# A decoder layer's SwiGLU halves: the down products of the four plain tiles moved directly behind them, in four parts instead of three

## The chip, the cores and the metric

The program runs on one core of one Trainium2 chip. The metric is the device time of one execution in microseconds (us). TensorE is PE in the profile (its weight loads PEld), VectorE is DVE, ScalarE is ACT, GpSimd is POOL, and SyncE is SP, which issues most of the loads.

## The reference

One layer over 512 tokens of width 1024, all in float32. The change lies in the two SwiGLU halves, one at each end of the layer; between them are the HGRN2 and convolution groups and the cross-attention.

```python
def swiglu(h, w_gate, w_up, w_down):
    return (jax.nn.silu(h @ w_gate) * (h @ w_up)) @ w_down

x = x + 0.5 * swiglu(rms_norm(x, ffn1_norm[l]), ffn1_gate[l], ffn1_up[l], ffn1_down[l])
...
x = x + 0.5 * swiglu(rms_norm(x, ffn2_norm[l]), ffn2_gate[l], ffn2_up[l], ffn2_down[l])
return rms_norm(x, final_norm)
```

The hidden width is 2816, which is 22 tiles of 128.

## The kernel before, in words

Every float32 operand is split in two parts that add up to it: a high part made by ACT (`whi`, `ah`, `a11h`, ...) and a low part made by DVE as the difference (`wlo`, `al`, `a11l`, ...). A product takes three matmuls: high by high, high by low, low by high (`mm3`, lines 119 to 121; line 339 for the block products). So each weight costs a load by DMA into a `raw` tile, a conversion by ACT and a subtraction by DVE. `wpool` has three buffers each of `raw`, `whi` and `wlo`; a `whi` buffer is written again once PE has done with it.

A half (`class Half`) makes its 22 hidden tiles in two ways. Tiles 0 to 3 are plain (`CLASSIC = 4`): `product(m, j)` multiplies the normed input by the gate weights (j = 0) or the up weights (j = 1), 24 matmuls of 512 columns, and `finish(m, ps)` scales by the row norm `bc`, applies silu, multiplies, and splits the result into the hidden tile (`ah`, `al`). Tiles 4 to 21 come in pairs from seven 2x2 block products (`seven(m)`: p1, p5, r6, p2, r7, p4, p3, each 24 matmuls of 256 columns). Their moving operands are combinations of the scaled input, made once per half by `inputs_steps()`: `xa` (line 253), `tx`, the differences q1 and n2, the combinations `tc`, and from these seven pairs of split inputs (`quad`, lines 242 and 243: a11, q1, n2, a12, d3, a22, q4). Their weights are five tiles per pair of hidden tiles, loaded by `load(m)` into six buffers with the tag `raw` in the pool `hp`: b11, t1 (loaded, then a second block added to it by a POOL DMA), b22, b21, t3 (a POOL load and a POOL add).

The down projection runs in parts of the hidden tiles (`PARTS`): `down_tile` loads the weights of one of the eight output tiles for one part, multiplies into a PSUM bank `psd`, and `residual` (line 192) adds the bank to `x` on DVE. [...] Before, the first part is hidden tiles 0 to 7, in the pair m = 8.

The order on each engine is set by the scheduler from the order of the code and its own estimates: an instruction may be put ahead of another, and from then on each engine works through its list strictly in order. In `run`, the plain tiles come first, the input steps stand among them, and the last input steps (`later`) stand among the first pair's seven products. In the first half a special `first_tile` makes three products at once while x arrives; the sum of squares of x (`Norm.add`) and two small mask loads (`mskf`, converted by DVE) stand behind it.

Of the kernel before, what the change touches and what calls it, by code (L numbers as in the profile page):

```python
# [8 lines left out]
F32 = mybir.dt.float32  # L9
# [29 lines left out]
def decoder_layer(ctx: ExitStack, tc: tile.TileContext, xT, memT, vecs, masks, ident_d,  # L39
                  w1, w1d, w_in, w_i, w_out, w_q, w_k, w_v, w_o, w2, w2d, gfin, out):  # L40
    nc = tc.nc
# [3 lines left out]
    tmp = ctx.enter_context(tc.tile_pool(name="tmp", bufs=2))  # L45
# [3 lines left out]
    def bank(name):  # L49
        return psp.tile([P, 512], F32, tag="ps", name=name)  # L50
# [65 lines left out]
    def mm3(out, wh, wl, xh, xl, first, last):  # L116


        nc.tensor.matmul(out, lhsT=wh, rhs=xh, start=first, stop=False)  # L119
        nc.tensor.matmul(out, lhsT=wh, rhs=xl, start=False, stop=False)  # L120
        nc.tensor.matmul(out, lhsT=wl, rhs=xh, start=False, stop=last)  # L121
# [69 lines left out]
    def residual(ps, k, scale):  # L191
        nc.vector.scalar_tensor_tensor(x[k], ps, scale, x[k], op0=ALU.mult, op1=ALU.add)  # L192


    CLASSIC = 4
    PARTS = ((0, 8), (8, 16), (16, FT))

    class Half:

# [46 lines left out]
        def inputs_steps(self):  # L246

            name, hp = self.name, self.hp
            self.q, later = {}, []
            sub = lambda o, a, b: nc.vector.tensor_tensor(o, a, b, ALU.subtract)  # L250

            def scaled(t, k):
                nc.vector.scalar_tensor_tensor(t, x[k], vec[:, self.gcol + k:self.gcol + k + 1], self.bc,
                                               op0=ALU.mult, op1=ALU.mult)

            self.tx = [hp.tile([P, 2, S], F32, tag=t, name=f"x{t}_{name}", bufs=4) for t in ("ah", "al")]
            self.tc = [hp.tile([P, 2, S], F32, tag=t, name=f"c{t}_{name}", bufs=4) for t in ("ah", "al")]
            steps = []
            for n in range(2):
                xb, comb = self.tx[n], self.tc[n]  # L260
                xa = []

                def one(n=n, xb=xb, xa=xa):
                    xa.append(hp.tile([P, 2, S], F32, tag="g", name=f"xa_{name}{n}", bufs=1))
                    for i in range(2):
                        scaled(xa[0][:, i], 2 * n + i)
                    self.quad("a11", n, xa[0][:, :, :256])

                def two(n=n, xb=xb, xa=xa):
                    for i in range(2):  # L270
                        scaled(xb[:, i], 4 + 2 * n + i)
                    q1 = tmp.tile([P, 2, 256], F32, tag="sq", name=f"q1_{name}{n}")
                    sub(q1, xa[0][:, :, 256:], xb[:, :, 256:])
                    self.quad("q1", n, q1)
                    n2 = tmp.tile([P, 2, 256], F32, tag="t2", name=f"n2_{name}{n}")
                    sub(n2, q1, xa[0][:, :, :256])
                    self.quad("n2", n, n2)
                    self.n2 = n2

                def three(n=n, xb=xb, comb=comb, xa=xa):  # L280
                    d3, q4 = comb[:, :, :256], comb[:, :, 256:]
                    sub(d3, xa[0][:, :, :256], xa[0][:, :, 256:])
                    nc.vector.tensor_tensor(q4, xb[:, :, :256], self.n2, ALU.add)
# [109 lines left out]
            return p1, p5, r6, p2, r7, p4, p3  # L393


        def run(self, first, down, fill, last):
# [12 lines left out]
            self.finish(2, p2)  # L409
            p3 = []  # L410
            for j in range(2):
                steps.pop(0)()
                steps.pop(0)()
                p3.append(self.product(3, j))
            self.finish(3, p3)
            for s in steps:
                s()
            before = None
            for m in range(CLASSIC, FT, 2):
                p1, p5, r6, p2, r7, p4, p3 = self.seven(m)  # L420
# [5 lines left out]
                for s in later[:2]:  # L426
                    s()
                r6()
                for s in later[2:4]:
                    s()  # L430
                part = [q for q, (a, b) in enumerate(PARTS) if b == m]
                if part:
                    down(part[0])
                p2()
                for s in later[4:6]:
                    s()
                r7()
                for s in later[6:]:
                    s()
                later = []  # L440
# [6 lines left out]
    def down_tile(half, name, d, part, src, n0=0, n1=None, p=None):  # L447
# [52 lines left out]
    with tc.tile_pool(name="hid1", bufs=1, reuse_waits="tile") as hp:  # L500
        half = Half("f1", hp, xs, norm, w1, V_FFN1)

        def src1(d, k0, k1):
            return w1d[d, :, k0 * P:k1 * P]

        def down1(part):
            for d in range(KT):
                down_tile(half, "f1", d, part, src1)

        L0, L1 = PARTS[-1]  # L510
        LATE = FT - 2
        psl = {}

        def early1(d):


            w = (LATE - L0) * P
            wh, wl = weights(w1d[d:d + 2, :, L0 * P:LATE * P].rearrange("d p c -> p d c"), (2, w))
            for i in range(2):
                p = psl[d + i] = bank(f"psd_f1l{d + i}")  # L520
                for k in range(L0, LATE):
                    hi, lo = half.hidden(k)
                    c = slice((k - L0) * P, (k - L0 + 1) * P)
                    mm3(p, wh[:, i, c], wl[:, i, c], hi, lo, k == L0, False)

        def fill1():
            early1(0)

        def last1():
            early1(2)  # L530
            wh, wl = weights(w1d[:4, :, LATE * P:].rearrange("d p c -> p d c"), (4, 2 * P))
            for d in range(4):
                for k in range(LATE, FT):
                    hi, lo = half.hidden(k)
                    c = slice((k - LATE) * P, (k - LATE + 1) * P)
                    mm3(psl[d], wh[:, d, c], wl[:, d, c], hi, lo, False, k == FT - 1)
                residual(psl[d], d, 0.5)
                done_m(d)
            for d in range(4, KT):
                down_tile(half, "f1", d, 2, src1)  # L540
                done_m(d)

        half.run(first_tile, down1, fill1, last1)


    norm_a, xs_a, done_a = prepare(V_XATT, "xa")
    with tc.tile_pool(name="mix", bufs=8, reuse_waits="tile") as mp:
# [26 lines left out]
        f = big("f")  # L574
# [92 lines left out]
        fill = []  # L667
# [297 lines left out]
    with tc.tile_pool(name="hid2", bufs=1, reuse_waits="tile") as hp:  # L965
# [3 lines left out]
        def src2(d, k0, k1):  # L969
            return w2d[k0:k1, :, d * P:(d + 1) * P].rearrange("k p c -> p k c")  # L970

        def down2(part):
            for d in range(KT):
                down_tile(half, "f2", d, part, src2)
# [9 lines left out]
        half.run(None, down2, fill2, lambda: None)  # L984
# [131 lines left out]
```

## Time and profile before

| what | value |
| --- | --- |
| runs shown | 1128.27 us median of 3 (1126.99 to 1129.56) |
| profiled execution, its own time | 1127.54 us |
| span of the profile, first to last instruction | 1125.8 us |
| mean granted TensorE clock | 0.990 |
| PE / DVE / ACT / POOL busy | 98% / 64% / 43% / 7% |
| DMA | 140.53 MB, mean 125 GB/s |

The time of the profiled execution is 1.7 us more than its span, and 0.7 us below the median of the runs. Times of rows are us from the span's start. A timeline row gives start, duration, engine, line, operation, output<-inputs, shapes and, in brackets, the idle time of the engine before it with what ended it. The matmul rows overlap, since matmuls are pipelined: what one costs in a stream is the distance from one start to the next.

### The profile page before, as it was taken

What the parts mean: (1) busy time and instruction counts of PE and PEld (TensorE: products, weight loads), DVE (VectorE), ACT (ScalarE), POOL (GpSimd) and SP (SyncE); (2) the same over time, 40 slices, a digit from 0 to 9 for tenths busy, and PEclk for the clock granted to TensorE, in tenths of its full rate; (3) what the DMA queues carried; (4) which work ended last, traced back from release to release, by engine and by line L of the source; (5) the groups of instructions that cost most, each with busy time, mean ns of one, the idle gap of its engine ahead of it and who ended that gap; (6) DMA issues with size and microseconds to landing.
All of it is one profiled execution on the core that took longest, in us unless ns stands there. A gap on an engine that the chain in (4) does not pass through costs nothing. (4 is left out here: it accounts for less than half of the span.)

```text
span 1125.8 us, 15892 instructions
## 1 busy us (share of the span) xinstructions
PE 1101.7 (98%) x6528; PEld 983.2 (87%) x6528; DVE 719.7 (64%) x956; ACT 486.1 (43%) x659; POOL 75.7 (7%) x75
## 2 busy tenths in 40 slices
PE   8979999999999999999999999999799999999997
PEld 6879889998998888888889888888699899988995
DVE  5797447754667575885776456553986366734744
ACT  6355325542445343323464345342654145523553
POOL 1001001100100000000100000000011011100102
PEclk9989999999999999999999999999999999999999
DMA  9428537773523322322234424732257357653521
GB/s 325 144 57 203 134 97 183 170 187 93 141 63 101 110 94 75 95 75 84 66 113 132 131 75 150 205 94 83 68 132 193 90 140 200 164 145 105 126 75 75
DMA packets 69641, 140.53 MB, mean 125 GB/s; under 512 B 4816, under 2 KB 22480, under 8 KB 69568
## 3 DMA queue, kind: packets, MB, share of 16 engines
q1 hardware_dynamic: 55008, 108.02, 31.1%
q0 software_dynamic: 12544, 28.84, 13.0%
q10 hardware_dynamic: 2016, 2.66, 0.7%
q8 instruction: 51, 0.84, 0.3%
q14 instruction: 22, 0.18, 0.0%
HBM read 137.40 MB, written 2.10 MB: 124 GB/s over the span
## 5 line engine op out<-in xcount | busy, mean ns | idle before, releaser
L110 ACT ACTIVATE whi<-raw 128x1024 fp32r<-128x1024 f32 (+4 forms) x135 | 136.5, 1016 | 337.4 <-PE psd_f L120 90.7
L111 DVE TENSOR_TENSOR wlo<-raw,whi 128x1024 fp32r<-128x1024 f32 (+4 forms) x135 | 157.2, 1168 | 87.8 <-ACT whi L110 87.4
L317 ACT ACTIVATE whi<-b_f 128x1024 fp32r<-128x1024 f32 x72 | 76.4, 1061 | 113.2 <-PE psd_f L120 35.0
L318 DVE TENSOR_TENSOR wlo<-b_f,whi 128x1024 fp32r<-128x1024 f32 x72 | 88.1, 1224 | 36.2 <-ACT whi L317 35.1
L119 PE MATMUL psd_f<-ah_f,whi 128*128 128x512 f32 x280 | 109.0, 389 | 0.0
L120 PE MATMUL psd_f<-al_f,whi 128*128 128x512 f32 x280 | 109.0, 389 | 0.0
L121 PE MATMUL psd_f<-ah_f,wlo 128*128 128x512 f32 x280 | 108.9, 389 | 0.0
L192 DVE SCALAR_TENSOR_TENSOR xall<-psd_f,xall 128x512 f32<-128x512 f32 x36 | 24.9, 692 | 103.6 <-PE psd_f L121 103.6
L318 DVE TENSOR_TENSOR wlo<-t_f,whi 128x1024 fp32r<-128x1024 f32 x54 | 66.1, 1224 | 36.7 <-ACT whi L317 36.7
L317 ACT ACTIVATE whi<-t_f 128x1024 fp32r<-128x1024 f32 x54 | 57.1, 1058 | 49.6 <-issue 20.8
L121 PEld LDWEIGHTS psd_f<-ah_f,wlo 128*128 128x128 f32 x280 | 52.6, 188 | 11.0
L119 PEld LDWEIGHTS psd_f<-ah_f,whi 128*128 128x128 f32 x280 | 52.6, 188 | 10.8
L120 PEld LDWEIGHTS psd_f<-al_f,whi 128*128 128x128 f32 x280 | 52.6, 188 | 10.7
L339 PE MATMUL psD_f<-q1h_f,wlo 128*128 128x256 f32 x144 | 42.8, 297 | 4.9 <-DVE wlo L318 4.9
L339 PE MATMUL psA_f<-a11h_f,whi 128*128 128x256 f32 x144 | 41.9, 291 | 5.6 <-ACT a11h_f L242 5.6
L339 PE MATMUL psA_f<-a11l_f,whi 128*128 128x256 f32 x144 | 42.2, 293 | 1.6 <-DVE a11l_f L243 1.6
L339 PE MATMUL psD_f<-q1l_f,whi 128*128 128x256 f32 x144 | 42.4, 295 | 0.0
L339 PE MATMUL psD_f<-q1h_f,whi 128*128 128x256 f32 x144 | 42.4, 295 | 0.0
L339 PE MATMUL psA_f<-a11h_f,wlo 128*128 128x256 f32 x144 | 41.9, 291 | 0.0
L339 PE MATMUL psA_f<-n2h_f,whi 128*128 128x256 f32 x144 | 40.9, 284 | 0.0
L339 PE MATMUL psA_f<-a22h_f,whi 128*128 128x256 f32 x144 | 40.8, 283 | 0.0
L339 PE MATMUL psA_f<-n2h_f,wlo 128*128 128x256 f32 x144 | 40.8, 283 | 0.0
(783 smaller groups left out, 3217.6 us busy)
## 6 DMA issues: line engine op xcount, KB each, us to landing
t_f<-in_w POOLq DMA_DIRECT2D x54, 512.0 KB, 5.9
b_f<-in_w SPq DMA_DIRECT2D x54, 512.0 KB, 4.4
raw<-in_w_in SPq DMA_DIRECT2D x24, 512.0 KB, 3.5
raw<-in_w2d SPq DMA_DIRECT2D x22, 512.0 KB, 3.5
raw<-in_w1d SPq DMA_DIRECT2D x19, 512.0 KB, 3.5
t_f<-in_w SPq DMA_DIRECT2D x18, 512.0 KB, 5.2
raw<-in_w SPq DMA_DIRECT2D x13, 512.0 KB, 3.6
raw<-in_w_out SPq DMA_DIRECT2D x8, 512.0 KB, 3.6
```

The lines of the kernel that those rows point to most:

```text
L110: nc.scalar.activation(hi[:, c], raw[:, c], AF.Copy)
L111: nc.vector.tensor_tensor(lo[:, c], raw[:, c], r32(hi[:, c]), ALU.subtract)
L119: nc.tensor.matmul(out, lhsT=wh, rhs=xh, start=first, stop=False)
L120: nc.tensor.matmul(out, lhsT=wh, rhs=xl, start=False, stop=False)
L121: nc.tensor.matmul(out, lhsT=wl, rhs=xh, start=False, stop=last)
L192: nc.vector.scalar_tensor_tensor(x[k], ps, scale, x[k], op0=ALU.mult, op1=ALU.add)
L317: nc.scalar.activation(hi, raw, AF.Copy)
L318: nc.vector.tensor_tensor(lo, raw, r32(hi), ALU.subtract)
L339: nc.tensor.matmul(o, lhsT=a[:, i, w], rhs=b, start=first and i == 0 and k == 0 and n == 0, stop=k == 3 and n == 2, skip_group_check=True)
```

## The change

The parts become 0 to 3, 4 to 9, 10 to 15 and 16 to 21. The first part is done by a new function, `down_pairs`, directly behind the fourth plain tile and ahead of the first block product: output tiles in four pairs, each pair with one weight load of 1024 columns, the three early hidden tiles of both first and the fourth hidden tile behind them, and three of the `later` input steps behind each pair. The input steps write to the six `raw` buffers of `hp` (`xa`, `qn`, `c` twice each) instead of `g`, the `ah`/`al` tags and temporaries, so the first `load(m)` now follows the release of these buffers.

```diff
-    PARTS = ((0, 8), (8, 16), (16, FT))
+    PARTS = ((0, 4), (4, 10), (10, 16), (16, FT))
...
+            raw = lambda key: hp.tile([P, 2, S], F32, tag="raw", name=f"{key}_{name}", bufs=6)
             self.tx = [hp.tile([P, 2, S], F32, tag=t, name=f"x{t}_{name}", bufs=4) for t in ("ah", "al")]
-            self.tc = [hp.tile([P, 2, S], F32, tag=t, name=f"c{t}_{name}", bufs=4) for t in ("ah", "al")]
+            tmps = [(raw(f"xa{n}"), raw(f"qn{n}")) for n in range(2)]
+            self.tc = [raw(f"c{n}") for n in range(2)]
...
             p2 = [self.product(2, 0)]
             self.bc = self.norm.rows()
+            p2.append(self.product(2, 1))
             steps, later = self.inputs_steps()
             self.finish(0, p0)
             self.finish(1, p1)
             steps.pop(0)()
-            p2.append(self.product(2, 1))
+            p3 = [self.product(3, 0)]
             self.finish(2, p2)
-            p3 = []
-            for j in range(2):
-                steps.pop(0)()
-                steps.pop(0)()
-                p3.append(self.product(3, j))
+            steps.pop(0)()
+            steps.pop(0)()
+            p3.append(self.product(3, 1))
+            steps.pop(0)()
             self.finish(3, p3)
-            for s in steps:
-                s()
+            steps += later
+            begin(steps)
...
+    def down_pairs(half, name, src, cut, steps):
+        k1 = PARTS[0][1]
+        for d in range(0, KT, 2):
+            wh, wl = weights(src(d), (src(d).shape[1], src(d).shape[2]))
+            ps = [bank(f"psd_{name}0_{d + i}") for i in range(2)]
+            for ks in (range(k1 - 1), range(k1 - 1, k1)):
+                for i in range(2):
+                    for k in ks:
+                        hi, lo = half.hidden(k)
+                        a, c = cut(i, k)
+                        mm3(ps[i], wh[:, a, c], wl[:, a, c], hi, lo, k == 0, k == k1 - 1)
+            for i in range(2):
+                residual(ps[i], d + i, 0.5)
+            for _ in range(3):
+                if steps:
+                    steps.pop(0)()
+        for s in steps:
+            s()
```

In `run` the `later` steps leave the first pair's seven products, and `down(part)` is called at m = 10 and m = 16.

Three places show how the instructions move. First, PE behind product(3, 1) of the first half. Before, the block products of pair 4 follow at once; `a11h_f_491` is made from the second `xa`, and `whi_563` is b11's high part:

```order
L121 MATMUL ps_f_1_515<-x_f17h,wlo_511 128x512
L339 MATMUL psA_f_562<-a11h_f_396,whi_563 128x256
L339 MATMUL psA_f_562<-a11l_f_397,whi_563 128x256
L339 MATMUL psA_f_562<-a11h_f_396,wlo_564 128x256
L339 MATMUL psA_f_562<-a11h_f_396,whi_563 128x256
L339 MATMUL psA_f_562<-a11l_f_397,whi_563 128x256
L339 MATMUL psA_f_562<-a11h_f_396,wlo_564 128x256
L339 MATMUL psD_f_593<-q1h_f_445,whi_594 128x256
L339 MATMUL psD_f_593<-q1l_f_446,whi_594 128x256
L339 MATMUL psA_f_562<-a11h_f_491,whi_563 128x256
```

Now 18 matmuls of the first pair of `psd` banks stand there (the three early hidden tiles, `ah_f_416` and the first half of `ah_f_471`), then eight early matmuls of banks 2 to 5, the last of which begins the piece below. Hidden tile 3 is the second half of `ah_f_471` and `al_f_472`; `whi_633`, `whi_679` and `wlo_588` belong to the third, fourth and second down weights:

```order
L120 MATMUL psd_f_5_639<-al_f_417,whi_633 128x512
L119 MATMUL psd_f_0_540<-ah_f_471,whi_535 128x512
L119 MATMUL psd_f_1_541<-ah_f_471,whi_535 128x512
L120 MATMUL psd_f_0_540<-al_f_472,whi_535 128x512
L121 MATMUL psd_f_0_540<-ah_f_471,wlo_536 128x512
L120 MATMUL psd_f_1_541<-al_f_472,whi_535 128x512
L121 MATMUL psd_f_1_541<-ah_f_471,wlo_536 128x512
L119 MATMUL psd_f_6_684<-ah_f_416,whi_679 128x512
L120 MATMUL psd_f_6_684<-al_f_417,whi_679 128x512
L119 MATMUL psd_f_7_685<-ah_f_416,whi_679 128x512
L120 MATMUL psd_f_7_685<-al_f_417,whi_679 128x512
L121 MATMUL psd_f_2_592<-ah_f_416,wlo_588 128x512
```

The block products stand 96 matmuls of 512 columns later; what PE meets ahead of them is hidden tile 3 and the splits of the down weights.

Second, DVE at the same place, from the low part of hidden tile 3 on. Before:

```order
L233 TENSOR_TENSOR al_f_438<-u_f_543,ah_f_437 128x512
L243 TENSOR_TENSOR n2l_f_506<-n_f_503,n2h_f_505 128x512
L250 TENSOR_TENSOR cal_f_374<-xa_f_488 128x2x256
L283 TENSOR_TENSOR cal_f_374<-xal_f_372,n_f_503 128x2x256
L318 TENSOR_TENSOR wlo_595<-t_f_551,whi_594 128x1024
L243 TENSOR_TENSOR a12l_f_623<-xah_f_371,a12h_f_622 128x512
```

Now, with the residuals of banks 0 and 1 ahead of the split of the second down weights, `wlo_588`:

```order
L233 TENSOR_TENSOR al_f_472<-u_f_529,ah_f_471 128x512
L250 TENSOR_TENSOR qn_f_407<-qn_f_407,xa_f_406 128x2x256
L243 TENSOR_TENSOR q1l_f_573<-qn_f_407,q1h_f_572 128x512
L192 SCALAR_TENSOR_TENSOR xall<-psd_f_0_540,xall 128x512
L192 SCALAR_TENSOR_TENSOR xall<-psd_f_1_541,xall 128x512
L281 TENSOR_TENSOR c_f_409<-xal_f_403,qn_f_407 128x2x256
L243 TENSOR_TENSOR n2l_f_579<-qn_f_407,n2h_f_578 128x512
L243 TENSOR_TENSOR a12l_f_583<-xah_f_402,a12h_f_582 128x512
L111 TENSOR_TENSOR wlo_588<-raw_586,whi_587 128x1024
L243 TENSOR_TENSOR a12l_f_621<-xal_f_403,a12h_f_620 128x512
```

Seven instructions now stand between hidden tile 3 and `wlo_588`, which PE needs ten matmuls after it first needs hidden tile 3; no split of a block weight stands here any more.

Third, SP's loads at the start of the program, behind the last loads of x. Before, loads for the block products (`b_f`, `t_f`; lines 304 to 308) stand among those of the plain tiles:

```order
L304 DMA b_f_550<-in_w 128x2x512
L106 DMA raw_287<-in_w 128x1024
L106 DMA raw_335<-in_w 128x1024
L106 DMA raw_400<-in_w 128x1024
L305 DMA t_f_551<-in_w 128x2x512
L307 DMA b_f_552<-in_w 128x2x512
L308 DMA b_f_553<-in_w 128x2x512
L304 DMA b_f_749<-in_w 128x2x512
L106 DMA raw_457<-in_w 128x1024
```

Now:

```order
L106 DMA raw_287<-in_w 128x1024
L106 DMA raw_335<-in_w 128x1024
L106 DMA raw_371<-in_w 128x1024
L106 DMA raw_434<-in_w 128x1024
L106 DMA raw_489<-in_w 128x1024
L104 DMA raw_534<-in_w1d 128x2x512
L104 DMA raw_586<-in_w1d 128x2x512
L104 DMA raw_632<-in_w1d 128x2x512
L104 DMA raw_678<-in_w1d 128x2x512
L303 DMA b_f_716<-in_w 128x2x512
```

The first load of a block product stands behind five loads of plain weights and the four of the down weights, and waits for a buffer of the input steps; on POOL's queue the t3 load that stood ahead of the norm's power, and the two adds into t1 and t3, now stand behind it.

More of the change, by code (lines that the diff above doesn't have):

```diff
@@ L260, in inputs_steps, with one, two, three @@
                 xb, comb = self.tx[n], self.tc[n]
[L261 to L264 removed]
+                xa, qn = tmps[n]
+                q1, n2 = qn[:, :, :256], qn[:, :, 256:]
+                def one(n=n, xa=xa):
                     for i in range(2):
[L266 to L269 removed]
+                        scaled(xa[:, i], 2 * n + i)
+                    self.quad("a11", n, xa[:, :, :256])
+                def two(n=n, xb=xb, xa=xa, q1=q1, n2=n2):
                     for i in range(2):
                         scaled(xb[:, i], 4 + 2 * n + i)
[L272 to L273 removed]
+                    sub(q1, xa[:, :, 256:], xb[:, :, 256:])
+                    sub(n2, q1, xa[:, :, :256])
                     self.quad("q1", n, q1)
[L275 to L276 removed]
+                def three(n=n, xb=xb, comb=comb, xa=xa, n2=n2):
+                    sub(comb[:, :, :256], xa[:, :, :256], xa[:, :, 256:])
+                    nc.vector.tensor_tensor(comb[:, :, 256:], xb[:, :, :256], n2, ALU.add)
                     self.quad("n2", n, n2)
[L278 to L283, printed above, removed]
                 steps += [one, two, three]
@@ L393, in seven, with run @@
             return p1, p5, r6, p2, r7, p4, p3
-        def run(self, first, down, fill, last):
+        def run(self, first, begin, down, fill, last):
             p0, p1 = first() if first else ([self.product(0, 0), self.product(0, 1)], [self.product(1, 0)])
@@ L425, in run @@
                 p5()
-                for s in later[:2]:
-                    s()
-                r6()
-                for s in later[2:4]:
-                    s()
-                part = [q for q, (a, b) in enumerate(PARTS) if b == m]
+                r6()
+                part = [q for q, (a, b) in enumerate(PARTS) if b == m and m > CLASSIC]
                 if part:
@@ L434, in run @@
                 p2()
-                for s in later[4:6]:
-                    s()
-                r7()
-                for s in later[6:]:
-                    s()
-                later = []
+                r7()
                 before = p4, p3
@@ L445, in run, with down_tile @@
             last()
-    def down_tile(half, name, d, part, src, n0=0, n1=None, p=None):
+    def down_pairs(half, name, src, cut, steps):
[16 more added lines that the diff above has]
+            s()
+    def down_tile(half, name, d, part, src):
         k0, k1 = PARTS[part]
@@ L504, in src1, with begin1 @@
             return w1d[d, :, k0 * P:k1 * P]
+        def begin1(steps):
+            down_pairs(half, "f1", lambda d: w1d[d:d + 2, :, :PARTS[0][1] * P].rearrange("d p c -> p d c"),
+                       lambda i, k: (i, slice(k * P, (k + 1) * P)), steps)
         def down1(part):
@@ L539, in last1 @@
             for d in range(4, KT):
-                down_tile(half, "f1", d, 2, src1)
+                down_tile(half, "f1", d, len(PARTS) - 1, src1)
                 done_m(d)
-        half.run(first_tile, down1, fill1, last1)
+        half.run(first_tile, begin1, down1, fill1, last1)
     norm_a, xs_a, done_a = prepare(V_XATT, "xa")
@@ L970, in src2, with begin2 @@
             return w2d[k0:k1, :, d * P:(d + 1) * P].rearrange("k p c -> p k c")
+        def begin2(steps):
+            down_pairs(half, "f2", lambda d: w2d[:PARTS[0][1], :, d * P:(d + 2) * P].rearrange("k p c -> p k c"),
+                       lambda i, k: (k, slice(i * P, (i + 1) * P)), steps)
         def down2(part):
@@ L982, in fill2 @@
                 nc.scalar.activation(x[k], ps, AF.Copy)
-        half.run(None, down2, fill2, lambda: None)
+        half.run(None, begin2, down2, fill2, lambda: None)
         gf = [xpool.tile([P, 512], F32, tag="xh", name=f"gf{j}", bufs=KT) for j in range(2)]
```

## The prediction

> **What bounds the kernel now.** I read the busy shares first, then the waits of PE, then PE's timeline at each wait, and then windows cut along the stages.
>
> ```profile
> PE 1101.7 (98%) x6528; PEld 983.2 (87%) x6528; DVE 719.7 (64%) x956; ACT 486.1 (43%) x659; POOL 75.7 (7%) x75
> ```
>
> PE is the bound and the change leaves it the same matmuls, so time can come only from where PE stands or runs slowly. The list of PE's waits (engine, line, releaser: total us, times, longest) is short:
>
> ```profile
> PE psA_f L339 <- ACT a11h_f L242: 5.6, 2, 2.8
> PE psD_f L339 <- DVE wlo L318: 4.9, 2, 2.6
> PE psA_f L339 <- DVE a11l_f L243: 1.6, 2, 0.8
> PE ps_f L119 <- ACT whi L110: 1.3, 1, 1.3
> PE psn_f L147 <- DVE acc_f L141: 1.1, 1, 1.1
> ...
> PE ps_f L121 <- DVE wlo L111: 0.5, 1, 0.5
> ```
>
> The first three come twice: once in each half, where the plain tiles pass into the block products. The last three come once, near 25 us, in the opening. The windows (columns: PE busy, PEld, DVE, ACT, POOL, granted clock, DMA share, GB/s) tell what they cost:
>
> ```profile
> 53.28:58.72 5.44, 5.44 (x25) 4.50 (x24) 5.44 (x9) 3.46 (x5) 1.23 (x1) 1.00 0.31 98
> 58.72:75.08 16.36, 10.11 (x52) 9.41 (x50) 16.36 (x25) 9.87 (x16) 0.00 (x0) 0.69 0.20 32
> 80.58:83.46 2.88, 2.88 (x26) 2.88 (x25) 1.82 (x2) 1.37 (x2) 0.27 (x1) 1.00 0.73 235
> 804.02:820.06 16.04, 10.12 (x55) 9.51 (x54) 16.04 (x25) 10.05 (x16) 0.11 (x1) 0.79 0.21 33
> ```
>
> A product of 24 matmuls of 512 columns takes 5.44 us (0.227 each), one of 256 columns 2.88 us (0.12 each); two of the counted matmuls in each window only run over its start. So 58.72 to 75.08 holds 50 starts, worth 6.0 us, in 16.4: 10.4 us lost. The second half loses 16.0 - 53 x 0.12 = 9.7 us. DVE is busy for the whole of both windows: it makes the inputs of the block products while PE waits. The loss is more than the waits, because the granted clock drops to 0.69 and 0.79. Cut into stretches of 3.41 us:
>
> ```profile
> 61.34:64.75 3.41, 1.24 (x8) 1.05 (x9) 3.41 (x6) 2.06 (x4) 0.00 (x0) 1.00 0.33 59
> 64.75:68.16 3.41, 2.46 (x13) 2.17 (x11) 3.41 (x7) 2.23 (x5) 0.00 (x0) 0.50 0.00 0
> 68.16:71.57 3.41, 1.73 (x8) 1.73 (x9) 3.41 (x5) 2.64 (x5) 0.00 (x0) 0.50 0.00 0
> 71.57:74.98 3.41, 3.41 (x18) 3.41 (x18) 3.41 (x5) 2.20 (x3) 0.00 (x0) 0.50 0.00 0
> 27.22:30.63 3.41, 2.06 (x12) 1.59 (x13) 3.20 (x10) 0.89 (x1) 0.34 (x1) 1.00 1.13 213
> 30.63:34.04 3.41, 3.41 (x10) 2.66 (x9) 1.84 (x2) 0.00 (x0) 1.61 (x1) 0.50 1.08 302
> ```
>
> A stretch in which PE was thinly busy (1.24 us; 2.06 us with eight one-column matmuls in it) is followed by a whole stretch at half clock, and a busy stretch ends that.
>
> **The opening (term A).** DMA from 20 to 26 us (total, and the mask load: KB each, us to landing), and from the page the landing of plain weights over the whole run:
>
> ```profile
> DMA packets 1199, 2.36 MB, mean 394 GB/s; under 512 B 99, under 2 KB 220, under 8 KB 1198
> ...
> mskf<-in_masks ACTq DMA_DIRECT2D x1, 256.0 KB, 6.3
> ```
>
> ```profile
> raw<-in_w_in SPq DMA_DIRECT2D x24, 512.0 KB, 3.5
> ```
>
> The timelines of DVE, ACT and PE:
>
> ```profile
> 21.59 1.48 DVE L141 TENSOR_TENSOR acc_f<-acc_f,sq_f 128x512 f32<-128x512 f32 x2
> 26.22 0.43 DVE L496 CAST msk<-mskf 128x512 uint8<-128x512 f32 x1 [3.15 <-DMA mskf<-in_masks]
> 26.56 1.48 DVE L141 TENSOR_TENSOR acc_f<-acc_f,sq_f 128x512 f32<-128x512 f32 x2
> ...
> 28.91 1.22 DVE L111 TENSOR_TENSOR wlo<-raw,whi 128x1024 fp32r<-128x1024 f32 x1
> ```
>
> ```profile
> 25.17 2.94 ACT L110 ACTIVATE whi<-raw 128x1024 fp32r<-128x1024 f32 x3
> ```
>
> ```profile
> 26.26 0.50 PE L119 MATMUL ps_f<-x_f10h,whi 128*128 128x512 f32 x1 [1.30 <-ACT whi L110]
> ...
> 28.10 1.05 PE L147 MATMUL psn_f<-inv_d,acc_f 128*128 128x1 f32 x8 [1.10 <-DVE acc_f L141]
> ...
> 30.18 0.50 PE L121 MATMUL ps_f<-x_f10h,wlo 128*128 128x512 f32 x1 [0.47 <-DVE wlo L111]
> ```
>
> DMA is full there, at 394 GB/s. The first mask load (256 KB) takes 6.3 us from issue, where a 512 KB weight in quiet times takes 3.5. DVE stands 3.15 us for it with the last two sums of squares behind it, and PE stands for these. In the change the loads for the block products (six of 512 KB that SP and POOL issue in the first 25 us, with two adds) are gone from here. The mask then lands about 3 us earlier, by the two landing times, and DVE goes on when the squares are there. The weight's high part stays ACT's matter: 25.17 plus a third of 2.94 is 26.2, and its 1.3 us wait stays. From 26.26 PE does two matmuls (0.7 us), the one-column group (0.9 us from start to next start) and two more (0.6 us), and would issue the row of 30.18 at 28.45; its low part is ready at 26.2 + 1.2 = 27.5. That is 1.7 us. With that much less standing the half-clock stretch at 30.63 probably goes: eight matmuls that start in it at 3.41 / 8 = 0.43 instead of 0.227, 1.6 us. A = 3.3. Bounds: 0 if the mask lands no earlier; 4.6 if x, too, arrives earlier by one such load (0.52 MB at 394 GB/s, 1.3 us). I take the mechanism without the last.
>
> **The passage in each half (terms B and C).** I walk DVE's new list from the last start that both lists share, with the spacing of rows there, in the first half's clock before A shifts it:
>
> ```profile
> 55.62 0.75 DVE L253 SCALAR_TENSOR_TENSOR xah_f<-xall,vec,rsb_f 128x512 f32<-128x512 f32 x1
> 56.29 0.69 DVE L250 TENSOR_TENSOR cah_f<-xa_f 128x512 f32<-128x512 f32 x1
> 56.89 0.69 DVE L250 TENSOR_TENSOR q_f<-xa_f,xah_f 128x512 f32<-128x512 f32 x1
> ...
> 68.56 1.23 DVE L318 TENSOR_TENSOR wlo<-t_f,whi 128x1024 fp32r<-128x1024 f32 x1
> ```
>
> ```profile
> 65.07 0.63 ACT L232 ACTIVATE ah_f<-u_f 128x512 fp32r<-128x512 f32 x1
> ...
> 68.62 0.61 ACT L242 ACTIVATE a22h_f<-xah_f 128x512 fp32r<-128x512 f32 x1
> 69.14 0.62 ACT L242 ACTIVATE a22h_f<-xal_f 128x512 fp32r<-128x512 f32 x1
> ```
>
> A scaled input takes 0.66 us, any other 512-column instruction 0.60, a weight split 1.23 to its end. PE ends product(3, 1) at 58.72 as before and goes on with 18 + 8 down matmuls: 26 x 0.227, to 64.6. Then it wants four things in turn.
> - Hidden tile 3, high: its input stands behind as much DVE work as before, so it comes as in the row at 65.07, ready at 65.7. PE stands 1.1 us.
> - Hidden tile 3, low: five scaled and eleven others from 55.62 are 9.9 us, plus 0.6 us where DVE waits for n2's high part (ACT's conversion of the third down weight, which waits for a buffer until PE ends product(3, 1), stands ahead of it). Start 66.1, ready 66.8: 0.7 us.
> - The fourth down weight, high: six conversions stand ahead of it on ACT, 0.52 to 0.6 us each from 65.1; one waits for the second n2 on DVE (67.4). It starts at 68.9 and is ready at 69.95: PE, done at 67.8, stands 2.1 us.
> - The second down weight, low: 24 instructions after 55.62 (five scaled, nineteen others, the 0.6 us), start 70.9, ready 72.2. PE has done four matmuls by 70.9 and stands 1.4 us.
>
> PE thus reaches 72.2 having issued 10 matmuls since 64.6: 7.6 - 2.3 = 5.3 us lost. No stretch of 3.4 us in there holds over 1.7 us of PE work, so by the stretches above one half-clock stretch follows, sometimes two; part of it falls into the waits, and what runs past 72.2 costs half its length: none to 2.8 us, and I take 1.5. The new passage loses 6.8.
>
> Behind it 60 down matmuls (13.6 us) cover DVE's remaining input steps, some 18 rows and 13 us; the splits of the third and fourth weights come at 75.1 and 79.5 against a need at 76.8 and 81.3. The block products' loads now wait for input buffers. The last, t3, starts when q4's first part is done, at 78.4. From the next unit's t3:
>
> ```profile
> 83.19 0.77 POOL L309 DMA_DIRECT2D t_f<-in_w  x1 [24.68 <-DVE b_f L325]
> ...
> 91.98 1.19 POOL L306 DMA_DIRECT2D t_f<-in_w  x1 [2.92 <-DMA t_f<-in_w]
> ```
>
> load and add take 8.8 us, so 87.2, and 89.5 split; PE wants it four block products after 85.9, at 97.4. Nothing waits there. B = 10.4 - 6.8 = 3.6. The second half has the same order and the same offsets (its a11h wait is also 2.8 us): C = 9.7 - 6.8 = 2.9.
>
> What is added: eight residuals per half at 0.60 us on DVE and four more weight splits of smaller size, under PE streams in which DVE had a quarter of its time free. Cost nothing; without that cover, 4.8 us per half. The loads move the same bytes.
>
> Sum: 3.3 + 3.6 + 2.9 = 9.8 us off the profiled execution's 1127.5 us: 1117.7, and 0.7 us more on the scale of the median, 1118.5.
>
> [...]
>
> **Rivals.**
> - Short gaps leave the clock alone after the passages: against it, the stretch at 27.22, with single gaps of 1.3 us and less. Without the 1.5 us twice, 1118.5 - 3.0 = 1115.5. [...]
> - The opening gains nothing, if the mask is slow for its own sake: against it, 394 GB/s in flight beside it. 1118.5 + 3.3 = 1121.8.
> - Only the opening gains: the passages lose as much as before, if ACT's list is later than I walked by 3 us. 1125.
> - Slower: DVE falls behind PE at each remaining pair of down products, so that PE stops and goes and stays at half clock. Place: `wlo` of the third and fourth pairs. Price: 60 matmuls x 0.2 = 12 us per half, 24 - 9.8 = 14 us over, 1142. It decides once these splits come over 1.5 us after PE's turn; I have them 1.7 us ahead, and a slow PE only widens that.
>
> **How the numbers follow.** Mine 0.52 (its own range 1115.5 to 1121.5), the full clock 0.15, no gain in the opening 0.18, the opening only 0.07, no change 0.03, slower 0.05. A change under 0.2% (2.3 us) can't be told from none here. Faster: 0.92; same 0.03; slower 0.05. The range 1112 to 1124 adds the bounds of A and of the clock on both sides.
>
> **What would show it.** PE's waits should name hidden tile 3 (`ah_f`, `al_f`) at `psd_f` with about 1 us each per half, then `whi` and `wlo` at lines 110 and 111 with about 2 and 1.4, and no a11h. The window from PE's last plain matmul to the first block product should last 96 x 0.227 + 6.8 = 28.6 us. The mask's wait on DVE should be gone. I am wrong if t3 or b21 appears among PE's waits, or if the half clock lasts over the later pairs.

## The result and the profile after

| kernel | median, us | runs | ratio to before, 95% interval |
| --- | --- | --- | --- |
| before | 1127.63 | 4 (1126.48 to 1129.56) | |
| after | 1117.59 | 4 (1117.26 to 1118.15) | 0.991 [0.9893, 0.9927] |

The change makes the kernel faster by 10.0 us, where 9.8 were forecast. The profiled execution of after took 1117.26 us with a span of 1115.5 us, 10.3 less than the span before. The busy shares of after (engine, busy us, share, instructions) show the same matmuls in 5.5 us less:

```profile
PE 1096.2 (98%) x6528; PEld 977.3 (88%) x6528; DVE 731.9 (66%) x980; ACT 486.5 (44%) x667; POOL 74.6 (7%) x75
```

PE's waits in after (line, releaser: total us, times, longest):

```profile
PE psd_f L119 <- ACT whi L110: 3.8, 2, 1.9
PE ps_f L119 <- ACT whi L110: 2.4, 2, 1.5
PE psd_f L121 <- DVE wlo L111: 2.1, 2, 1.1
PE psd_f L119 <- ACT ah_f L232: 1.5, 2, 0.7
...
PE psd_f L120 <- DVE al_f L233: 0.8, 2, 0.4
```

The waits at the block products are gone; the waits at `psd_f` are the four that the walk named, once in each half. The rows of PE, ACT and DVE at the first passage (start, duration, engine, line, operation, tiles, and in brackets the idle time ahead with its releaser):

```profile
60.34 0.73 PE L119 MATMUL psd_f<-ah_f,whi 128*128 128x512 f32 x2 [0.73 <-ACT ah_f L232]
61.49 0.50 PE L120 MATMUL psd_f<-al_f,whi 128*128 128x512 f32 x1 [0.41 <-DVE al_f L233]
64.58 0.50 PE L119 MATMUL psd_f<-ah_f,whi 128*128 128x512 f32 x1 [1.91 <-ACT whi L110]
66.83 0.80 PE L121 MATMUL psd_f<-ah_f,wlo 128*128 128x512 f32 x1 [1.04 <-DVE wlo L111]
...
809.78 0.79 PE L121 MATMUL psd_f<-ah_f,wlo 128*128 128x512 f32 x1 [1.06 <-DVE wlo L111]
```

```profile
63.48 1.04 ACT L110 ACTIVATE whi<-raw 128x1024 fp32r<-128x1024 f32 x1
```

```profile
60.75 0.68 DVE L233 TENSOR_TENSOR al_f<-u_f,ah_f 128x512 fp32r<-128x512 f32 x1
...
65.56 1.21 DVE L111 TENSOR_TENSOR wlo<-raw,whi 128x1024 fp32r<-128x1024 f32 x1
```

The windows of the two passages, and stretches of 3.41 us in the first (columns: PE busy, PEld, DVE, ACT, POOL, granted clock, DMA share, GB/s):

```profile
53.56:83.24 29.68, 25.59 (x98) 19.62 (x96) 26.09 (x38) 10.91 (x16) 3.25 (x3) 0.88 0.60 180
796.51:825.12 28.61, 24.51 (x97) 18.91 (x96) 26.07 (x38) 10.90 (x16) 3.16 (x3) 0.94 0.64 186
62.31:65.72 3.41, 1.50 (x6) 0.67 (x4) 3.41 (x7) 2.79 (x5) 0.00 (x0) 1.00 0.95 142
65.72:69.13 3.41, 2.37 (x6) 1.82 (x6) 3.41 (x5) 0.00 (x0) 0.00 (x0) 0.50 1.05 385
69.13:72.55 3.42, 3.42 (x10) 2.65 (x9) 1.79 (x3) 0.00 (x0) 0.00 (x0) 0.50 0.53 164
```

The 96 down matmuls would take 96 x 0.2267 = 21.76 us. They take 29.68 and 28.61, so the passages lose 7.9 and 6.85 us, where 10.4 and 9.7 were lost before. The first passage now starts at 53.56 instead of 58.72: the opening gave 5.16 us. 5.16 + 2.5 + 2.85 = 10.5, which is the span's 10.3 within 0.2.

The opening in after, PE and then DVE:

```profile
24.83 0.50 PE L119 MATMUL ps_f<-x_f10h,whi 128*128 128x512 f32 x1 [0.96 <-ACT whi L110]
...
25.41 0.95 PE L147 MATMUL psn_f<-inv_d,acc_f 128*128 128x1 f32 x8
...
26.76 0.39 PE L121 MATMUL ps_f<-x_f10h,wlo 128*128 128x512 f32 x1
```

```profile
22.01 0.43 DVE L508 CAST msk<-mskf 128x512 uint8<-128x512 f32 x1 [0.37 <-DMA mskf<-in_masks]
22.35 1.48 DVE L141 TENSOR_TENSOR acc_f<-acc_f,sq_f 128x512 f32<-128x512 f32 x2
```

DVE's wait for the mask fell from 3.15 to 0.37 us (its 256 KB landed 3.6 us after their issue, where they took 6.3), the one-column group no longer waits for the squares, and the low part of the weight, for which PE waited at 30.18, is used at 26.76. DMA issues between 1 and 14 us, of before and then of after (KB each, us to landing), show what the prediction had left out:

```profile
xall<-in_xT SPq DMA_DIRECT2D x3, 512.0 KB, 8.5
```

```profile
xall<-in_xT SPq DMA_DIRECT2D x3, 512.0 KB, 7.6
```

From issue to landing the large loads of x take 0.9 us less. The runs below bear this out: 8.5 us in e2_early, where the early loads stand in the opening, and 7.7 us in e1_gate, where they don't.

### The profile page after: what moved, and what is told of

Read it like the earlier page. It is cut to its first block, busy times and chain, and to the rows that moved or that the text cites. A ratio compares the mean times of both kernels' runs of the same rounds, so it can differ in the third digit from the quotient of the medians.

```text
span 1115.5 us, 15978 instructions
## 1 busy us (share of the span) xinstructions
PE 1096.2 (98%) x6528; PEld 977.3 (88%) x6528; DVE 731.9 (66%) x980; ACT 486.5 (44%) x667; POOL 74.6 (7%) x75
## 5 line engine op out<-in xcount | busy, mean ns | idle before, releaser
L192 DVE SCALAR_TENSOR_TENSOR xall<-psd_f,xall 128x512 f32<-128x512 f32 x52 | 35.5, 689 | 76.8 <-PE psd_f L121 76.8
L338 PE MATMUL psA_f<-d3l_f,whi 128*128 128x256 f32 x144 | 40.8, 283 | 0.0
L338 PE MATMUL psD_f<-q4l_f,whi 128*128 128x256 f32 x144 | 40.8, 283 | 0.0
```

Of the source, the lines that this page charges most:

```text
L338: nc.tensor.matmul(o, lhsT=a[:, i, w], rhs=b, start=first and i == 0 and k == 0 and n == 0, stop=k == 3 and n == 2, skip_group_check=True)
```

## Experiments

My theory: the early loads of pair 4 had slowed the opening, and in each passage DVE has a backlog of input steps; the change gives PE other work meanwhile, and what is still lost depends on the order in which DVE works the backlog off. The rivals stand in each expectation. The times of before in the runs' own comparisons are 1127.17, 1126.62 and 1126.59 us (medians of 19, 9 and 7 runs), so times of different comparisons can differ by about 1 us for no reason in the kernel.

| kernel | median, us | ratio to before, 95% interval |
| --- | --- | --- |
| e1_gate (before, early loads delayed) | 1125.50 | 0.9989 [0.9979, 0.9998] |
| e1b_gate_early (the same, delayed less) | 1123.10 | 0.9964 [0.9952, 0.9977] |
| e2_early (after, early loads put back) | 1122.26 | 0.9960 [0.9945, 0.9975] |
| e3_parts (before with four parts) | 1127.40 | 1.0001 [0.9991, 1.0010] |
| e4_finish (after, tile 3 first) | 1117.63 | 0.9921 [0.9905, 0.9938] |
| e5_first (e4 and weight splits first) | 1109.54 | 0.9843 [0.9827, 0.9858] |
| e6_late (e5 and six steps later) | 1107.35 | 0.9828 [0.9813, 0.9842] |
| e7_load (e6 and pair 4's loads first) | 1102.94 | 0.9794 [0.9778, 0.9811] |

### e1_gate: the kernel before without the early loads

```diff
+            if self.name == "f1":
+                for i in range(6):
+                    gate = self.hp.tile([P, 2, S], F32, tag="raw", name=f"gate{i}", bufs=6)
+                    nc.vector.tensor_copy(gate[:, 0, :1], self.bc[:, :1])
             steps, later = self.inputs_steps()
```

> The kernel before, with nothing of the change in it but this: in the first half the six buffers that the first block loads go to are first written by DVE, one column each, from the norm row, which exists near 38 us. So b11, t1, b22, b21, t3 and the next b11 cannot be loaded in the opening. Theory (the early block loads slow the opening, by 5.2 us at the end of product(3,1): 58.72 before, 53.56 after): 1127.6 - 5.2 = 1122.4 us, DVE's wait for mskf under 0.5 us, no half-clock stretch near 30 us, the two passages as before (10.4 and 9.7 us lost). Rival 1 (the opening gains from the order of the plain products in run, not from the loads): 1127.6. Rival 2 (only the size I forecast, 3.3 us): 1124.3.

Measured: 1125.50 us, 1.7 less than before, where 5 less were expected. The opening did what the theory said: DVE no longer waits for the mask, and the granted clock is 1.00 from 20 to 38 us. PE's wait for the weight and its first block product:

```profile
25.04 0.50 PE L119 MATMUL ps_f<-x_f10h,whi 128*128 128x512 f32 x1 [0.81 <-ACT whi L110]
...
53.76 0.28 PE L339 MATMUL psA_f<-a11h_f,whi 128*128 128x256 f32 x1
```

The passage starts at 53.76 instead of 58.72, 4.96 us sooner, with none of the order of after. But the passage gave part of it back. ACT's row for t1, and PE's wait behind it:

```profile
54.51 1.06 ACT L317 ACTIVATE whi<-t_f 128x1024 fp32r<-128x1024 f32 x1 [3.92 <-DMA t_f<-in_w]
```

```profile
56.65 0.38 PE L339 MATMUL psD_f<-q1h_f,whi 128*128 128x256 f32 x1 [2.02 <-ACT q1h_f L242]
```

t1 is loaded and then added to, and released near 40 us it landed at 54.5. ACT stood 3.92 us for it with q1's high part behind it. In the profiled runs 2.4 of the 4.96 us were lost again (spans 1125.8 and 1123.2); the 3.3 in the next expectation is the same difference by the medians.

### e1b_gate_early: the same, with the loads released sooner

```diff
-                    nc.vector.tensor_copy(gate[:, 0, :1], self.bc[:, :1])
+                    nc.vector.tensor_copy(gate[:, 0, :1], rst[:, :1])
```

> As e1_gate, with the six buffers written from the norm's power (near 28 us) and not from the norm row (near 39 us), so the block loads start some 10 us sooner and still behind the opening. In e1_gate product(3,1) ended at 53.76 us, 4.96 earlier than before, but t1 with its two-stage load landed at 54.5 us; ACT stood 3.92 us for it with q1h behind, and 3.3 us were given back in the passage. Theory (the early loads cost the opening 5 us, and in e1_gate their lateness cost 3.3): t1 lands near 44 us, no wait of ACT for it, product(3,1) ends near 53.8 us, the passage as before: 1122.4 us. Rival (a sooner end of the opening is always given back in the first passage, since DVE's backlog there ends at the same time): 1125.5 as in e1_gate.

Measured: 1123.10 us, 3.5 less than before; the rival's 1125.5 is out, and the theory's 1122.4 is met within 0.7. The wait for t1 is gone: ACT converts it at 49.55 us, having waited for PE and not for the load. The passage starts at 55.01 and not at 53.8, because a half-clock stretch fell into the opening. Stretches of 3.41 us of this kernel:

```profile
22.69:26.10 3.41, 2.40 (x16) 1.81 (x14) 2.70 (x7) 3.40 (x5) 0.00 (x0) 1.00 0.00 0
26.10:29.51 3.41, 3.41 (x9) 2.67 (x9) 2.98 (x12) 0.39 (x1) 1.04 (x1) 0.50 0.63 177
```

and PE's row in it:

```profile
24.65 0.50 PE L119 MATMUL ps_f<-x_f10h,whi 128*128 128x512 f32 x1 [1.01 <-ACT whi L110]
```

PE waited 1.01 us here, 0.81 in e1_gate and 0.96 in after; in these two the clock stayed at 1.00 from 20 to 40 us.

### e2_early: the kernel after with the early loads put back

```diff
+            if self.name == "f1":
+                self.early(CLASSIC)
             steps, later = self.inputs_steps()
...
+            e = [self.hp.tile([P, 2, 512], F32, tag="raw", name=f"early{i}", bufs=6) for i in range(6)]
+            nc.sync.dma_start(e[0], src(m, 0, 0))
+            nc.sync.dma_start(e[1], src(m, 0, 0))
+            nc.gpsimd.dma_start(e[1], src(m, 1, 0), accum_op=ALU.add)
+            nc.sync.dma_start(e[2], src(m, 1, 1))
+            nc.sync.dma_start(e[3], src(m, 0, 1))
+            nc.gpsimd.dma_start(e[4], src(m, 1, 0))
+            nc.gpsimd.dma_start(e[4], src(m, 1, 1), accum_op=ALU.add)
+            nc.sync.dma_start(e[5], src(m + 2, 0, 0))
```

> The kernel after, with the six early block loads of the kernel before put back into the opening (into the same six buffers, ahead of the input steps; nothing reads them, and pair 4 is loaded again later, so 4.2 MB more move). Theory: the opening loses its 5.2 us again, product(3,1) ends near 58.7 us, the passages stay as after (7.9 and 6.9 us lost): 1117.6 + 5.2 = 1122.8 us. Rival 1 (order of the plain products): 1117.6. Rival 2 (3.3 us): 1120.9.

Measured: 1122.26 us against 1122.8 expected. PE's rows:

```profile
25.99 0.50 PE L119 MATMUL ps_f<-x_f10h,whi 128*128 128x512 f32 x1 [1.29 <-ACT whi L110]
27.48 1.05 PE L147 MATMUL psn_f<-inv_d,acc_f 128*128 128x1 f32 x8 [0.75 <-DVE acc_f L141]
29.56 0.79 PE L121 MATMUL ps_f<-x_f10h,wlo 128*128 128x512 f32 x1 [0.46 <-DVE wlo L111]
```

The three waits of the opening before are back, with a half-clock stretch behind them (0.50 from 29.13 to 32.54 us); DVE waits 2.79 us for the mask, and the passage starts at 57.88, 4.3 us later than in after. Its four waits are those of after (0.73, 0.41, 1.89, 1.04 us). So the loads alone make nearly all of the opening's 5.16 us (4.3 by this run, 4.96 by e1_gate), and what is left against before, 4.9 us, is the passages' share.

### e3_parts: four parts alone

```diff
-    PARTS = ((0, 8), (8, 16), (16, FT))
+    PARTS = ((0, 4), (4, 10), (10, 16), (16, FT))
...
-                down_tile(half, "f1", d, 2, src1)
+                down_tile(half, "f1", d, len(PARTS) - 1, src1)
```

> The kernel before with the four parts alone: PARTS of 4, 6, 6 and 6 tiles, the first part done tile by tile in the first pair's seven products behind r6, where the kernel before calls down. Input steps, loads and opening are those of before. Theory (added residuals and splits are covered, and parts alone bring nothing since PE waits ahead of r6): 1127.6, within 1126.5 to 1129.5, with the waits for a11h, a11l and wlo of t1 as before. Rival 1 (the eight more residuals and eight more weight splits per half are not covered: 4.8 us per half): 1137. Rival 2 (a first part of four tiles already gives PE work in the passage): 1122 by the 2.5 and 2.9 us of the two passages.

Measured: 1127.40 us, ratio 1.0001. PE's waits are those of before:

```profile
PE psA_f L339 <- ACT a11h_f L242: 5.6, 2, 2.8
PE psD_f L339 <- DVE wlo L318: 4.1, 2, 2.2
...
PE psA_f L339 <- DVE a11l_f L243: 1.6, 2, 0.8
```

Sixteen more residuals and sixteen more weight splits cost nothing that can be measured, and the parts alone bring nothing. The gain of the passages comes from where the first part stands and from the order of the input steps around it, which the change moves too; no run separates these two. PE's rows in after show the first at work: 26 down matmuls run from 53.56 on, where before PE stood after eight block matmuls.

### e4_finish: hidden tile 3 two steps sooner

```diff
             steps.pop(0)()
-            steps.pop(0)()
             p3.append(self.product(3, 1))
-            steps.pop(0)()
             self.finish(3, p3)
+            steps.pop(0)()
+            steps.pop(0)()
```

> The kernel after with the finish of hidden tile 3 ahead of two input steps instead of behind them. DVE walked with the rows of after: u at 54.2, al at 57.3 us, where PE wants it at 57.6. Theory (DVE's backlog sets the passage, in whatever order it is worked off): the waits for ah, al and for the high part of the fourth down weight go, but wlo of the second down weight, behind two residuals and nine input instructions, is ready at 67.5 against a need at 62.0, so one wait of 5.5 us takes their place, with half clock behind it: 1117.6 us, within 1115 to 1120. Rival (PE waits for tile 3 itself, and what it releases; wlo moves up with it): 1.1 + 1.9 us per half come back, 1111.6.

Measured: 1117.63 us. PE's only waits in the two passages:

```profile
66.69 0.80 PE L121 MATMUL psd_f<-ah_f,wlo 128*128 128x512 f32 x1 [5.07 <-DVE wlo L111]
...
808.44 0.79 PE L121 MATMUL psd_f<-ah_f,wlo 128*128 128x512 f32 x1 [5.07 <-DVE wlo L111]
```

Four waits became one, of the same worth: the two passages lose 6.7 and 7.8 us (28.45 and 29.54 us for the 96 matmuls) where after loses 7.9 and 6.85. The instruction that DVE did last was another one. Taking away the waits that a list names does not pay when the releasing engine has as much to do as before ahead of the next need.

### e5_first: what PE wants first is done first

The edit of e4_finish, and in `down_pairs`:

```diff
+        get = lambda d: weights(src(d), (src(d).shape[1], src(d).shape[2]))
+        ready = [get(0), get(2)]
         for d in range(0, KT, 2):
-            wh, wl = weights(src(d), (src(d).shape[1], src(d).shape[2]))
+            wh, wl = ready.pop(0)
...
+            if d + 4 < KT:
+                ready.append(get(d + 4))
             for i in range(2):
                 residual(ps[i], d + i, 0.5)
```

> The kernel after with what PE wants first put first on DVE and ACT: the finish of hidden tile 3 ahead of two input steps (as in e4_finish), and each down weight split two pairs ahead, before residuals and input steps. DVE walked with the rows of after: al at 58.4 (need 59.0), wlo of the second weight at 51.8 (need 62), of the third 59.7 (need 65), of the fourth 68.1 (need 70.6), but then residuals and eight later input steps stand ahead of the split of b11, which is ready at 78.6 against a need at 75.6. Theory (DVE's backlog of about 3 us has to end somewhere; the waits inside the down products go and one wait of 3 us for wlo of b11 comes, with 0 to 2 us of half clock): 3 to 5 us lost per passage instead of 7.9 and 6.9, so 1117.6 - 7 = 1110.6 us, within 1107 to 1113. Rival (whatever is first, the same backlog is paid as in e4_finish): 1117.6.

Measured: 1109.54 us against 1110.6. The down products now start at 53.59 and end at 75.35: 21.76 us, nothing lost, and the same in the second half (792.43 to 814.19). The waits stand behind them, at the block products:

```profile
77.20 0.39 PE L338 MATMUL psD_f<-q1h_f,whi 128*128 128x256 f32 x1 [1.45 <-ACT whi L316]
78.03 0.39 PE L338 MATMUL psA_f<-a11h_f,wlo 128*128 128x256 f32 x1 [0.33 <-DVE wlo L317]
...
815.59 0.39 PE L338 MATMUL psD_f<-q1h_f,whi 128*128 128x256 f32 x1 [1.01 <-ACT whi L316]
816.87 0.39 PE L338 MATMUL psA_f<-a11h_f,wlo 128*128 128x256 f32 x1 [0.78 <-DVE wlo L317]
```

and windows of this kernel behind them:

```profile
79.35:81.35 2.00, 2.00 (x12) 2.00 (x10) 1.03 (x1) 0.86 (x1) 1.20 (x1) 0.50 1.02 369
818.19:820.19 2.00, 2.00 (x19) 2.00 (x18) 1.02 (x1) 0.87 (x1) 1.19 (x1) 1.00 1.01 349
```

The backlog left over is 1.8 us in each half instead of the 3 us that I had walked.

### e6_late: six input steps back among the first pair's products

```diff
-            steps += later
-            begin(steps)
+            a12, d3, a22, q4 = (later[i:i + 2] for i in range(0, 8, 2))
+            begin(steps + [d3[0], q4[0]])
+            later = [a12, [q4[1], d3[1]], a22]
...
                 p5()
+                for s in (later.pop(0) if later else []):
+                    s()
                 r6()
```

(the same two lines stand behind r6 and p2).

> As e5_first, and six of the eight later input steps (a12 twice, d3 and q4 of the second pair, a22 twice) go back among the seven products of the first pair, as in the kernel before; d3 and q4 of the first pair stay ahead, since their buffer is the one that t3 is loaded into. DVE walked: split of b11 ready at 73.4 (need 75.6), of t1 at 75.8 (need 78.2), of t1 + b22 at 81.2 (need 81.1). Theory (the remaining loss is only DVE's order, no longer its amount): every wait of the passage goes but about 0.5 us, and with them the half clock; 96 matmuls pass in 21.8 to 22.5 us, so 1117.6 - 7.4 - 6.5 = 1103.7 us, within 1102 to 1106. Rival (the stalls move on into the first pair's block products, since DVE has as much to do there): 3 us per half at t1 + b22 or d3, 1109.7.

Measured: 1107.35 us, outside my 1102 to 1106 and between theory and rival. The down products and the first two block products run without a wait; then PE's rows at r6, ACT's at t1 and SP's loads:

```profile
81.51 0.38 PE L338 MATMUL psA_f<-n2h_f,whi 128*128 128x256 f32 x1 [0.35 <-ACT whi L316]
83.30 0.39 PE L338 MATMUL psA_f<-n2h_f,wlo 128*128 128x256 f32 x1 [1.29 <-DVE wlo L317]
```

```profile
75.65 1.06 ACT L316 ACTIVATE whi<-t_f 128x1024 fp32r<-128x1024 f32 x1 [5.59 <-DMA t_f<-in_w]
```

```profile
52.34 8.22 SPq L106 DMA_DIRECT2D raw<-in_w1d  x2
...
61.08 0.47 SPq L304 DMA_DIRECT2D t_f<-in_w  x1
```

The first row covers two loads of later down weights: the second waited 7.4 us for a buffer at the head of SP's queue (the list of SP's waits), with pair 4's loads behind it. I had walked DVE and ACT and not SP.

### e7_load: pair 4's loads ahead in the code

```diff
+            early = self.load(CLASSIC)
             begin(steps + [d3[0], q4[0]])
...
-                st["raw"] = self.load(m)
+                st["raw"] = raw or self.load(m)
```

(`seven` takes these tiles for the first pair.)

> As e6_late, with the loads of pair 4 placed in the code ahead of the down products, so that on SP only one load of later down weights stands ahead of them instead of two (in e6_late the second of these waited for a buffer until 60.6 us, and t1, which is loaded and added to, landed at 75.7 us; DVE stood 2.79 us for it, and PE then 1.64 us at t1 + b22 in the first half). Theory (what e6_late still lost is this landing): t1 lands near 70 us, the split of t1 + b22 is ready at 78 us against a need at 81.1, both waits at r6 go; b11 of the next pair now comes last, ready at 89.8 against a need at 89.7, so 0 to 1 us is left there: 1107.4 - 2.5 = 1104.9 us, within 1103 to 1107. Rival (DVE has too much to do in the first pair whatever lands when): a wait of 1.3 to 1.6 us at another weight of the first pair, 1107.4.

Measured: 1102.94 us, a shade under the expected 1103 to 1107, 14.7 us less than after's 1117.59 (13.9 by the spans of the profiles, 1101.6 and 1115.5). PE's longest waits of the whole program, without the start-up's 1.1; the first line is the opening's:

```profile
PE ps_f L119 <- ACT whi L110: 2.2, 2, 1.4
...
PE psA_f L338 <- ACT sV_f L344: 0.3, 1, 0.3
```

No wait is left in either passage. t1 is converted at 70.31 and the split of t1 + b22 done at 78.5 us. This version beats both kernels; nearly all that the change still lost in the passages was order, first DVE's and then SP's.

## Why the prediction was right, point by point

**A, the opening: 3.3 forecast, 5.16 measured.** The mechanism held (e2_early, e1_gate); the size was short. By rows of before and after: the mask's and the squares' part, from the first matmul after the wait to the low-part matmul, 30.18 - 26.26 = 3.92 against 26.76 - 24.83 = 1.93, so 1.99 (1.7 forecast); the half-clock stretch, from there to the passage, 28.54 against 26.80, so 1.74 (1.6 forecast); and the rest, 26.26 against 24.83, 1.43 us. This last is the term that I bounded at 1.3 and left out: the loads of x take less time once the six loads no longer stand in DMA with them (8.5 us with them in e2_early, 7.7 without them in e1_gate). The step that failed is "I take the mechanism without the last": not only the mask's load was slower beside the six loads (6.3 us from issue to landing in before, 3.6 in after), those of x were too.

**B, the first passage: 3.6 forecast, 2.5 measured.** The walk of DVE and ACT held to 0.3 us. Shifted by A, it had the fourth down weight's conversion at 63.7 (63.48 measured), the second's low part at 65.7 (65.56), `al` ready at 61.6 (61.43). At 66.83 PE had issued 36 matmuls since 53.56: 13.27 - 36 x 0.2267 = 5.1 us lost, where 5.3 were forecast. What was mis-sized is the half clock: 7.9 - 5.1 = 2.8 us and not 1.5, since two stretches followed, and 5.7 us of them lay behind the last wait. That is the upper end of the range that I gave.

**C, the second passage: 2.9 forecast, 2.85 measured.** The same 5.1 us at the waits, and 6.85 - 5.1 = 1.7 us of half clock: here one stretch followed. That B has two and C one I put down to where the waits ended (see the last section): B's last at 66.83 us, inside its half clock (from 65.70), C's at 809.78, ahead of it (from 809.81). So there is some luck in how well C came out.

**The costs at nothing** held: e3_parts for the residuals and splits. No wait for t3 or b21 came. ACT's row for t3 in after:

```profile
89.12 1.06 ACT L316 ACTIVATE whi<-t_f 128x1024 fp32r<-128x1024 f32 x1 [1.33 <-PE psD_f L338]
```

ACT waited for a buffer that PE held, not for the load; PE began the block products at 83.24 and wanted t3 four products (11.5 us) later, at 94.8. But the prediction's 8.8 us for t3's load and add is a misreading. Its row at 91.98 (line 306) is the add into the next unit's t1, and it waited for that t1's load. The add into t3 and its use, in before:

```profile
87.86 1.20 POOL L310 DMA_DIRECT2D t_f<-in_w  x1 [3.91 <-DMA t_f<-in_w]
...
96.04 1.06 ACT L317 ACTIVATE whi<-t_f 128x1024 fp32r<-128x1024 f32 x1 [0.63 <-DMA t_f<-in_w]
```

From 83.19 to 96.04 are 12.85 us. Put in place of the 8.8, they bring t3 at 91.25 and its split at 93.5, still ahead of 97.4, so the cost at nothing did not hang on this reading.

**The rivals.** Short gaps did not leave the clock alone: no gap of after's passages is over 1.91 us, and both passages had half clock (0.50 from 65.70 to 72.53 and from 809.81 to 813.22). The opening's gain was real, and so was the passages' (e2_early keeps 4.9 us without the opening). DVE did not fall behind at the third and fourth pairs: their splits ended at 69.7 and 76.8 (69.9 and 74.3 by the walk, shifted), and PE waited for neither; the 1.5 us at which I let this rival decide was an estimate, which no run tried. That the forecast saving of 9.8 us came so near the measured 10.0 owes something to A and B missing in opposite directions, by 1.9 and 1.1.

**What I did not see**: the 6.9 to 7.9 us that the new passages still lose were not the price of the backlog, only of its order. The walk had what was needed to see it: it put seven instructions that nobody needed yet between hidden tile 3 and the low part of the second down weight. Four of the seven belong to the last two steps ahead of the `later` ones (`two` and `three` of the second pair), which `down_pairs` does as well.

## What to carry to other kernels

Where an engine with a backlog feeds the bound engine, list what the bound engine wants in order of time, and check that the feeder, and the queue that issues its loads, work in that order; moving one late item up (e4_finish) only hands its wait to the next. Give every load that nobody needs yet a buffer that comes free later: a prefetch into free buffers took 5 us (5.16 by before and after, 4.96 by e1_gate) from an opening in which DMA moved 394 GB/s from 20 to 26 us. But release a load with two stages early enough, or what it won is given back (2.4 of the 4.96 us in e1_gate).

## What the runs showed of the hardware

A short wait of the same length brought a half-clock stretch in one half and none in the other (e5_first). In the opening and the passages of after the granted clock changed at 65.70, 72.53, 809.81 and 813.22 us: the last two are 3.41 us apart, and the first lies 2, 218 and 219 steps of 3.413 us ahead of the others (747.52 us by 219). The changes of before at 30.63, 34.04, 64.76 and 75.00 us lie 1, 10 and 13 such steps behind the first. In e5_first the two halves waited 1.78 and 1.79 us at the same place; behind the first the clock was 0.50, behind the second 1.00. Counted in these steps from the fall of the clock in this run, at 78.67 us, the first half's waits fell into one stretch, which was left with 1.64 us of PE work (75.25 to 78.67); the second half's were spread over two, with 2.41 and 2.63 us (812.53 to 819.36).

From the first block product to the `psz` matmul on `x_mx2l` (360.2 us in e5_first, 364.3 in after) the first half then took 284.85 us, where after takes 281.06: 3.8 lost, 2.0 more than the waits. The second half, up to the end of the span, lost 2.2 (292.6 against 290.4), 0.4 more than its waits. The difference, 1.6 us, is my estimate of what one stretch costs in full work; half of 3.41 would be 1.7. In the first half of e4_finish PE did nothing at all for one whole stretch, and one stretch at half clock followed, most of it behind the wait:

```profile
62.70:66.11 3.41, 0.00 (x0) 0.00 (x0) 3.41 (x6) 3.41 (x7) 0.00 (x0) 1.00 1.01 174
66.11:69.52 3.41, 2.83 (x7) 2.25 (x8) 3.41 (x6) 0.23 (x1) 0.00 (x0) 0.50 0.94 301
```

In its second half two followed the same wait (806.79 to 813.62 by the steps; behind the wait PE's rows start 0.43 us apart up to 813.30, and 0.227 apart later). Over both halves the one long gap cost about as much as the four short ones of after: the passages lost 14.5 us in all against 14.8.

In the passages of after 1.91 us was the longest gap, and the clock still fell to 0.50 in both. Of the stretches at full clock, those left with 1.50 us of PE work (first half of after) and 1.64 (first half of e5_first) were followed by half clock, and so was one with 2.40 us with eight one-column matmuls in it (e1b_gate_early, 22.69 to 26.10); one with 1.92 us was not (after, 802.98 to 806.40). Of the stretches at half clock, those with 1.77 us (second half of e4_finish) and 2.37 us (first half of after) were followed by another; those with 2.83 us (first half of e4_finish) and 3.41 us (second half of after, 809.81 to 813.22) were not. So in these passages a thin stretch at half clock was followed by a second one, and a busy one was not. Where exactly the borders lie, no run here was made to find.
